# Feed-forward pairs of an encoder trunk: products joined in PSUM banks that ScalarE fills beforehand, in a new order

## The chip, the cores and the metric

One core of one Trainium2 chip runs the whole program. The metric is the device time of one execution in microseconds (us). The kernel before was run three times: 2769.55, 2768.38 and 2768.38 us, median 2768.38. The profile is one further execution, whose span from the first to the last instruction is 2767.2 us.

## The reference

Two sequences (512 and 256 tokens, 1024 wide) go through two layers with shared weights. Each layer is a feed-forward block, a token mixer and a second feed-forward block. There are thus four feed-forward blocks, and the change is in them alone.

```python
def swiglu_ffn(x, w1, w2):
    gate, up = jnp.split(x @ w1, 2, axis=-1)
    return (jax.nn.silu(gate) * up) @ w2

for li in range(DEPTH):
    x = x + 0.5 * swiglu_ffn(rmsnorm(x, norm_g[li, 0]), ffn_w1[li, 0], ffn_w2[li, 0])
    h = rmsnorm(x, norm_g[li, 1])
    ...
    x = x + mix
    x = x + 0.5 * swiglu_ffn(rmsnorm(x, norm_g[li, 2]), ffn_w1[li, 1], ffn_w2[li, 1])
```

Everything is in float32, `D_MODEL` is 1024 and `D_FF` is 2816, which is 22 columns of 128 hidden units.

## The kernel before, in words

**Tiling.** The 768 tokens of both sequences are handled together, in two halves of 384 (`H`). A float32 product is made of three matmuls: each operand is split into a rounded part and a remainder ("hi" and "lo"), and hi·hi, hi·lo and lo·hi are added up in PSUM. Splitting a weight takes a cast on ScalarE (L208), which gives hi, and a subtraction on VectorE (L209), which gives lo; for the product p5 of an up pair, GpSimd does the subtraction.

**Seven products instead of eight.** Most of the matmul work is done as a two-by-two block product by seven products p1 to p7 (Strassen's way, in Winograd's form). The first matrix is split by tokens and by the contracted dimension, the weights by gate/up and by the contracted dimension; the sums and differences of blocks that the seven products need are made beforehand. One column `j` of hidden units is one call of `up_pair`: seven products of 12 matmuls each (128x128 weights against 384 columns) into four PSUM banks a, b, c and d, and out come two tiles, silu(gate)·up of the two halves of the tokens. Columns 0 and 1 are done plainly (`up_plain`); the remaining 20 are pairs, so there are 80 pairs in the four blocks.

**Order in a block.** A block has five groups of four columns. After the columns of a group stands one `down_quad`: seven products with `w2`, each of 3 x 6 matmuls against 512 columns, 126 in all, whose results VectorE adds to the residual x (L599, by `add_x`). The down products run in the order `DOWN` = p1 p2 p5 p4 p7 p6 p3. p2, p4 and p3 run on in the banks of p1, p5 and p7, after VectorE has added what those banks held so far to x: p3 cannot begin in a bank of p7 before that addition. After the fifth group come the last two columns, as pairs, and their part of the down product (`add`).

**Weights.** `load_next` issues the loads on SP's queue into four raw buffers `wr` of 512 KB. For an up pair, raw buffer one holds blocks a11 and a12, buffer two holds a21 and a22. Three sums are made on the way: a DMA from GpSimd's queue adds a11 to a separately loaded block `s3` (for p7) and another adds a22 to a21 (`into`, L147); VectorE then makes a11 += a21 (the step "second" in the code) and a12 += a11 ("fourth"), both on L215. The table `UP` is the order in which an up pair's seven weights are staged; "second" and "fourth" are tied to a place in it by the dictionary `behind`. `ahead` stages as many weights as the eight buffers `w` hold: an up weight takes one of them, a down weight two, so a weight is staged up to eight products before it is used. It is called after each product, and behind a product's end its buffer comes free.

**Who sets the order.** The code emits operations in its own order; the framework then places them on each engine, where they run strictly in turn. `keep_in_program_order` holds "second" and "fourth" where the code has them. [...]

## Time and profile before

| what | value |
|---|---|
| median of three runs | 2768.38 us |
| span of the profiled execution | 2767.2 us |
| VectorE busy | 2206.5 us (80%), 3766 instructions |
| ScalarE busy | 1386.0 us (50%), 2589 instructions |
| GpSimd busy | 453.0 us (16%), 491 instructions |
| moved by DMA | 325.22 MB, 118 GB/s on average |
| mean granted TensorE clock | 0.999 |

How to read the rows: a group's row names the line of the code, the engine, the operation, what is written and read, and the count; then the busy time in us and the mean duration of one in ns; behind the second bar the time in which the engine was idle just before these instructions, and who ended the idle time. A row of waits names who waited for whom, with the total in us, the number of times and the longest. In the timeline a row gives the start in us, the duration in us, and in brackets the idle time before it.

### The profile page before, as it was taken

To read this page: it belongs to the slowest core of one execution; us is meant where nothing else is said; L and a number is where in the kernel's file an instruction comes from. 1 tells how busy PE (TensorE), PEld (TensorE's weight loads), DVE (VectorE), ACT (ScalarE), POOL (GpSimd) and SP (SyncE) were. 2 spreads that over 40 slices of the span, in tenths; PEclk is the share of its full clock that TensorE was granted. 3 is DMA by queue.
4 is the path that set the end of the run, shared out by engine and by line. 5 is a ranking of instruction groups with operands and counts; after the bars stand their busy time and mean duration, and the time that the engine had idled before them with its cause. 6 is when DMAs were issued, how large, how long until landed. Compare 5 with 4: busy or idle time off the path is not lost.

```text
span 2767.2 us, 40933 instructions
## 1 busy us (share of the span) xinstructions
PE 2745.0 (99%) x15117; PEld 2554.8 (92%) x15117; DVE 2206.5 (80%) x3766; ACT 1386.0 (50%) x2589; POOL 453.0 (16%) x491
## 2 busy tenths in 40 slices
PE   8999999999999999999999999999999999999998
PEld 8999999989999889999999999999888889999998
DVE  8788788767887888788878887887847868788877
ACT  7344444634455675444445543444458855444443
POOL 2111121200000101211111121111105611211111
PEclk9999999999999999999999999999999999999999
DMA  6554554851122743655444355544424422655443
GB/s 172 130 125 114 126 140 124 227 161 39 39 62 66 205 119 78 143 134 131 115 117 121 78 145 134 126 119 118 130 73 111 89 69 73 145 134 130 114 118 107
DMA packets 352040, 325.22 MB, mean 118 GB/s; under 512 B 14216, under 2 KB 271200, under 8 KB 351840
## 3 DMA queue, kind: packets, MB, share of 16 engines
q1 hardware_dynamic: 303040, 224.56, 27.7%
q0 software_dynamic: 44496, 84.56, 17.4%
q10 hardware_dynamic: 4304, 13.49, 1.3%
q8 instruction: 118, 1.93, 0.3%
q14 instruction: 82, 0.67, 0.1%
HBM read 225.82 MB, written 15.73 MB: 87 GB/s over the span
## 4 chain that ended last, share of the span: by engine, by line
PE 96%; DVE 2%; ACT 1%; DMA 1%; issue 0%; DVEq 0%; POOL 0%; SPq 0%; ACTq 0%; POOLq 0%
PE ps L513 42%; PE ps L577 21%; PE ps L315 6%; PE ps L316 6%; PE ps L314 6%; PE ps L760 5%; PE ps L823 3%; PE ps L928 1%; PE ps L1414 1%; PE ps L904 1%; PE ps L385 1%; PE ps L1426 0%; PE ps L1376 0%; PE ps L1427 0%; PE ps L1377 0%; PE ps L1181 0%
## 5 line engine op out<-in xcount | busy, mean ns | idle before, releaser
L513 PE MATMUL ps<-big,w 128*128 128x384 f32 x6720 | 1169.3, 334 | 0.0
L513 PEld LDWEIGHTS ps<-big,w 128*128 128x128 f32 x6720 | 1165.9, 188 | 1.7 <-ACT tA L530 0.2
L208 ACT CAST w<-wr 128x512 fp32r<-128x512 f32 x600 | 415.8, 707 | 689.2 <-PE ps L513 274.9
L577 PE MATMUL ps<-w,big 128*128 128x512 f32 x2520 | 575.7, 390 | 0.0
L577 PEld LDWEIGHTS ps<-w,big 128*128 128x128 f32 x2520 | 472.7, 188 | 98.0 <-ACT big L319 0.4
L209 DVE TENSOR_TENSOR w<-wr,w 128x512 fp32r<-128x512 f32 (+1 forms) x520 | 438.0, 846 | 145.9 <-ACT w L208 123.9
L147 POOL DMA_DIRECT2D s<-wr x126 | 109.8, 878 | 1250.3 <-DMA s<-in_ffn_w_dram 432.0
L599 DVE SCALAR_TENSOR_TENSOR x<-ps,x 128x512 f32<-128x512 f32 x468 | 302.4, 686 | 10.1 <-PE ps L316 10.0
L314 PE MATMUL ps<-big,w 128*128 128x384 f32 x640 | 219.6, 345 | 1.2 <-ACT w L175 0.9
L315 PE MATMUL ps<-big,w 128*128 128x384 f32 x640 | 215.7, 337 | 0.7 <-DVE big L320 0.7
L316 PE MATMUL ps<-big,w 128*128 128x384 f32 x640 | 214.6, 335 | 0.0
L319 ACT CAST big<-tA 128x384 fp32r<-128x384 f32 x296 | 148.0, 513 | 115.4 <-DVE tA L545 37.0
L147 POOL DMA_DIRECT2D wr<-wr x109 | 94.9, 871 | 518.3 <-DMA wr<-in_ffn_w_dram 165.9
L760 PE MATMUL ps<-w,big 128*128 128x512 f32 x756 | 177.1, 392 | 0.1
L320 DVE TENSOR_TENSOR big<-tA,big 128x384 fp32r<-128x384 f32 x296 | 168.0, 578 | 6.7 <-ACT big L319 4.7
L209 POOL TENSOR_TENSOR w<-wr,w 128x512 fp32r<-128x512 f32 x80 | 137.4, 1718 | 197.8 <-ACT w L208 195.8
L760 PEld LDWEIGHTS ps<-w,big 128*128 128x128 f32 x756 | 140.6, 188 | 29.1 <-DVE w L320 0.6
L215 DVE TENSOR_TENSOR wr<-wr,wr 128x512 f32<-128x512 f32 (+1 forms) x120 | 123.3, 1027 | 25.9 <-issue 23.6
L314 PE MATMUL ps<-w,big 128*128 128x512 f32 x336 | 134.6, 401 | 0.1
L316 PE MATMUL ps<-w,big 128*128 128x512 f32 x336 | 131.8, 392 | 0.5 <-DVE big L400 0.5
L315 PE MATMUL ps<-w,big 128*128 128x512 f32 x336 | 131.8, 392 | 0.0
L315 PEld LDWEIGHTS ps<-big,w 128*128 128x128 f32 x640 | 120.6, 188 | 2.0 <-DVE big L320 1.7
(214 smaller groups left out, 3504.0 us busy)
## 6 DMA issues: line engine op xcount, KB each, us to landing
wr<-in_ffn_w_dram SPq DMA_DIRECT2D x264, 512.0 KB, 4.0
s<-wr POOLq DMA_DIRECT2D x126, 256.0 KB, 4.8
s<-in_ffn_w_dram SPq DMA_DIRECT2D x120, 256.0 KB, 3.2
wr<-wr POOLq DMA_DIRECT2D x80, 256.0 KB, 3.8
wr<-in_hg_w_in_dram SPq DMA_DIRECT2D x32, 512.0 KB, 3.9
wr<-wr POOLq DMA_DIRECT2D x29, 512.0 KB, 4.6
spill<-x ACTq DMA_DIRECT2D x12, 512.0 KB, 4.0
kept<-big POOLq DMA_DIRECT2D x8, 768.0 KB, 9.7
```

Of the source, the lines that this page charges most:

```text
L147: self.nc.gpsimd.dma_start(out, src, accum_op=ALU.add)
L208: nc.scalar.copy(h, src)
L209: (eng or nc.vector).tensor_sub(l, src, h.bitcast(F32))
L314: nc.tensor.matmul(out, a[0], b[0], start=first, stop=False)
L315: nc.tensor.matmul(out, a[0], b[1], start=False, stop=False)
L316: nc.tensor.matmul(out, a[1], b[0], start=False, stop=last)
L319: self.nc.scalar.copy(hi, src)
L320: self.nc.vector.tensor_sub(lo, src, hi.bitcast(F32))
L513: self.nc.tensor.matmul(ps, a[x], b[y], start=first and k == 0 and i == 0, stop=k == 3 and i == 2, skip_group_check=True,)
L577: nc.tensor.matmul(ps, a[x], w[y], start=name == chain and kp == 0 and q == 0, stop=kp == 1 and q == 2, skip_group_check=True,)
L599: self.nc.vector.scalar_tensor_tensor(x, ps, c, x, ALU.mult, ALU.add)
L760: nc.tensor.matmul(ps, x[:, sl], y, start=fresh and k == 0 and q == 0, stop=k == 3 and q == 2, skip_group_check=True,)
```

## The change

The seven products of `up_pair` run in the order p1 p5 p6 p2 p7 p3 p4 instead of p1 p7 p2 p5 p4 p6 p3, and the results are joined differently. Before, every product or pair of products stood in a bank of its own, and VectorE joined them with five additions and subtractions, then two multiplications. Now ScalarE writes −p1 into bank b, and p6's matmuls add to it there; ScalarE copies that bank into bank c, and p7 and then p4 add to it there. VectorE is left with two subtractions and two multiplications per pair. ScalarE has six operations per pair instead of four. The first pair behind the plain columns takes the two banks in which the plain columns were made.

In staging, "second" moves from behind p5 to behind p1, and "fourth" from behind p4 to behind p2. The second half of the tokens now comes out of a pair first, and in the last columns the block (2, 0) is added ahead of (0, 1).

```diff
-UP = ("p1", "p7", "p2", "p5", "p4", "p6", "p3")
+UP = ("p1", "p5", "p6", "p2", "p7", "p3", "p4")
...
+    def seeded(self):
+        return self.wide.pop(0) if self.wide else self.ps(H)
...
-        behind = {"p5": "second", "p4": "fourth"} if up else {}
+        behind = {"p1": "second", "p2": "fourth"} if up else {}
...
+        if half and j == PLAIN - 1:
+            self.wide += pss
         return t
...
-        a, b, c, d = (self.ps(H) for _ in range(4))
-        v, w, t = (self.tmp(H) for _ in range(3))
+        a, d = (self.ps(H) for _ in range(2))
+        b, c = (self.seeded() for _ in range(2))
+        t, v, w = (self.tmp(H) for _ in range(3))
         p = lambda name, ps, first, last: self.product(key, name, FACTOR[name], ps, first, last)
         p("p1", a, True, False)
-        nc.scalar.copy(v, a)
+        nc.scalar.activation(b, a, AF.Copy, scale=-1.0)
         self.ahead()
-        p("p7", c, True, False)
-        nc.scalar.copy(w, c)
+        p("p5", d, True, False)
+        nc.scalar.copy(w, d)
+        self.ahead()
+        p("p6", b, False, True)
+        nc.scalar.copy(c, b)
+        nc.scalar.copy(v, b)
         self.ahead()
         p("p2", a, False, True)
-        nc.scalar.activation(a, a, AF.Silu)
+        nc.scalar.activation(t, a, AF.Silu)
         self.ahead()
-        p("p5", d, True, False)
-        nc.vector.tensor_sub(w, w, d)
+        p("p7", c, False, False)
+        nc.vector.tensor_sub(w, c, w)
+        self.ahead()
+        p("p3", d, False, True)
+        nc.vector.tensor_sub(v, d, v)
+        self.last_act = nc.scalar.activation(v, v, AF.Silu).ins
+        nc.vector.tensor_mul(w, v, w)
+        yield 1, w
         self.ahead()
         p("p4", c, False, True)
-        p("p6", b, True, True)
-        nc.vector.tensor_sub(v, v, b)
-        nc.vector.tensor_sub(t, c, v)
-        nc.vector.tensor_mul(t, t, a)
-        yield t
-        nc.vector.tensor_sub(w, w, v)
-        self.ahead()
-        p("p3", d, False, True)
-        nc.vector.tensor_add(v, v, d)
-        self.last_act = nc.scalar.activation(v, v, AF.Silu).ins
-        self.last_dve = nc.vector.tensor_mul(w, v, w).ins
-        yield w
+        self.last_dve = nc.vector.tensor_mul(t, c, t).ins
+        yield 0, t
         self.ahead()
...
-            for i, k in (((0, 0), (1, 0), (0, 1)), ((1, 1),))[b] if b < 2 else ((b, 0), (b, 1)):
+            for i, k in (((0, 0), (1, 0), (2, 0), (0, 1)), ((1, 1),), ((2, 1),))[b] if b < 3 else ((b, 0), (b, 1)):
```

Lines from L82 on stand lower in the code after the change, by 4 up to the pairs and by 7 from the down products on: L208, L209 and L215 become L212, L213 and L219, L319 and L320 become L323 and L324, L434 becomes L438, and L599 becomes L606.

Two places show what the change does to the queues. The first is VectorE in the second half of a down product, while the weights of the next group's first pair are staged; `wr_1411` and `wr_1412` are that pair's two raw buffers, `ps_1433` to `ps_1435` the three banks of the down product p7, `ps_1438` to `ps_1440` those of p6, and L215 on 128x512 with two buffers is "second". Before:

```order
L599 SCALAR_TENSOR_TENSOR x_1236_8687<-ps_1428_9980,x_1236_8687 128x512
L209 TENSOR_TENSOR w_1431_10014<-wr_1411_9853,w_1431_10014 128x512
L209 TENSOR_TENSOR w_1432_10017<-s3_1413_9857,w_1432_10017 128x512
L599 SCALAR_TENSOR_TENSOR x_1249_8769<-ps_1433_10020,x_1249_8769 128x512
L599 SCALAR_TENSOR_TENSOR x_1250_8771<-ps_1434_10028,x_1250_8771 128x512
L599 SCALAR_TENSOR_TENSOR x_1251_8773<-ps_1435_10036,x_1251_8773 128x512
L209 TENSOR_TENSOR w_1436_10044<-wr_1411_9853,w_1436_10044 128x512
L215 TENSOR_TENSOR wr_1411_9853<-wr_1411_9853,wr_1412_9855 128x512
L599 SCALAR_TENSOR_TENSOR x_1249_8769<-ps_1438_10051,x_1249_8769 128x512
```

The same place after the change, where the raw buffers are `wr_1514` and `wr_1515`, p7's banks `ps_1536` to `ps_1538`, and p6's first bank `ps_1541`:

```order
L606 SCALAR_TENSOR_TENSOR x_1234_8665<-ps_1531_10731,x_1234_8665 128x512
L213 TENSOR_TENSOR w_1534_10765<-wr_1514_10595,w_1534_10765 128x512
L606 SCALAR_TENSOR_TENSOR x_1247_8747<-ps_1536_10772,x_1247_8747 128x512
L219 TENSOR_TENSOR wr_1514_10595<-wr_1514_10595,wr_1515_10597 128x512
L606 SCALAR_TENSOR_TENSOR x_1248_8749<-ps_1537_10780,x_1248_8749 128x512
L606 SCALAR_TENSOR_TENSOR x_1249_8751<-ps_1538_10788,x_1249_8751 128x512
L213 TENSOR_TENSOR w_1539_10796<-wr_1514_10595,w_1539_10796 128x512
L213 TENSOR_TENSOR w_1540_10799<-wr_1514_10595,w_1540_10799 128x512
L606 SCALAR_TENSOR_TENSOR x_1247_8747<-ps_1541_10803,x_1247_8747 128x512
```

"Second" now stands ahead of the additions from the second and third bank of p7, where it stood behind all three. It stands so in all 20 down products.

The second place is ScalarE while the third pair of a group runs, when the sums of the two earlier pairs' hidden tiles (`mix`) are split too; `big` are split hidden tiles, `w` weights, `ps` banks. Before, from the copy of p1 on:

```order
L530 COPY tA_1490_10404<-ps_1486_10400 128x384
L208 CAST w_1493_10420<-s3_1464_10231 128x512
L319 CAST big_1480_10378<-tA_1471_10258 128x384
L533 COPY tA_1491_10405<-ps_1488_10402 128x384
L208 CAST w_1494_10436<-wr_1462_10227 128x512
L319 CAST big_1482_10386<-tA_1453_10122 128x384
L536 ACTIVATE ps_1486_10400<-ps_1486_10400 128x384
L208 CAST w_1495_10452<-wr_1463_10229 128x512
L319 CAST big_1483_10391<-tA_1472_10259 128x384
```

After, from the filling of bank b (L537) to that of bank c (L543):

```order
L537 ACTIVATE ps_1484_10375<-ps_1482_10373 128x384
L212 CAST w_1489_10393<-wr_1458_10201 128x512
L323 CAST big_1478_10359<-tA_1450_10098 128x384
L540 COPY tA_1488_10379<-ps_1483_10374 128x384
L212 CAST w_1490_10409<-wr_1457_10199 128x512
L323 CAST big_1479_10364<-tA_1466_10231 128x384
L323 CAST big_1480_10367<-tA_1468_10233 128x384
L323 CAST big_1481_10370<-tA_1448_10096 128x384
L543 COPY ps_1485_10376<-ps_1484_10375 128x384
```

L530 and L533 wrote temporaries in SBUF. L537 and L543 write the banks into which p6 and p7 add, and four casts of hidden tiles stand between them.

More of the change, by code (lines that the diff above doesn't have):

```diff
@@ L65, in __init__ @@
         self.uid = 0
+        self.wide = []
         self.deferred = []
@@ L610, in gather @@
             def gather(ts, kp):
-                self.mix(ts[0], ts[1], ts[2], ts[3], lambda name, src: put(name, src, kp))
+                self.mix(*(ts[i] for i in range(4)), lambda name, src: put(name, src, kp))
             if g == 0:
@@ L625, in ffn @@
                     continue
-                ts = []
+                ts = {}
                 for j in range(2):
-                    for half, t in enumerate(self.up_pair(tag, 4 * g + 2 * kp + j)):
-                        ts.append(t)
+                    for half, t in self.up_pair(tag, 4 * g + 2 * kp + j):
+                        ts[2 * j + half] = t
                         name = f"b{j}{half}"
@@ L637, in ffn @@
             hid = self.big([P, 2, T], F32R)
-            for half, t in enumerate(self.up_pair(tag, j)):
+            for half, t in self.up_pair(tag, j):
                 self.split(t, *(hid[:, i, half * H : (half + 1) * H] for i in range(2)))
```

## The prediction

> **What bounds the kernel now.** I read the page first, then who TensorE waits for, then TensorE in a stretch of two feed-forward blocks.
>
> ```profile
> span 2767.2 us, 40933 instructions
> PE 2745.0 (99%) x15117; PEld 2554.8 (92%) x15117; DVE 2206.5 (80%) x3766; ACT 1386.0 (50%) x2589; POOL 453.0 (16%) x491
> ```
>
> ```profile
> PE ps L116 <- DMA tB<-in_hg_g_norm_dram: 7.6, 1, 7.6
> PE ps L1376 <- ACT tA L1367: 1.3, 2, 1.1
> ...
> PE ps L1426 <- ACT tA L319: 0.2, 1, 0.2
> ```
>
> ```profile
> 1062.00:1987.00 925.00, 924.94 (x4936) 871.25 (x4935) 753.10 (x1204) 415.98 (x723) 147.37 (x146) 1.00 0.51 123
> L513 PE MATMUL ps<-big,w 128*128 128x384 f32 x6720 | 1169.3, 334 | 0.0
> ```
>
> TensorE is busy for all but 22.2 us of the span. It waits in twelve places, the longest for the first constants (7.6 us), then 1.3 us and less, and none of the twelve is a pair's matmul on L513. In the 925 us window of two feed-forward blocks TensorE is busy 924.94 us at a granted clock of 1.00. The 6720 matmuls of the pairs take 1169.3 us, 174 ns each, with no idle time before them. VectorE is busy 753.10 of the same 925 us, and nothing in the pairs waits for it for long. TensorE sets the time alone.
>
> **What the change removes.** The number of matmuls stays: seven products of 12, 80 times. Three VectorE operations per pair go and two ScalarE operations come.
>
> ```profile
> L543 DVE TENSOR_TENSOR tA<-tA,ps 128x384 f32<-128x384 f32 x80 | 44.1, 551 | 37.8 <-PE ps L513 37.6
> L539 DVE TENSOR_TENSOR tA<-tA,ps 128x384 f32<-128x384 f32 x80 | 44.1, 552 | 78.6 <-PE ps L513 78.6
> L533 ACT COPY tA<-ps 128x384 f32<-128x384 f32 x80 | 38.4, 480 | 83.2 <-PE ps L513 82.9
> L536 ACT ACTIVATE ps<-ps 128x384 f32<-128x384 f32 x80 | 38.0, 475 | 57.8 <-PE ps L513 57.8
> ACT tA L533 <- PE ps L513: 82.9, 76, 1.7
> ```
>
> VectorE loses 240 x 0.55 = 132 us, ScalarE gains 160 x 0.48 = 77 us. All of it lay beside matmuls: L539, L543 and L533 wait for TensorE (78.6, 37.8 and 83.2 us in all), not TensorE for them. So the saving is worth nothing on the path, and the extra 77 us on an engine that is 50% busy cost nothing in themselves. No copy from one bank to another stands in the trace; L536, which writes back to a bank, takes 475 ns, as long as L533 to SBUF, so I take 0.48 us.
>
> **What the change adds: three new waits.** TensorE now waits for two ScalarE operations in each pair, and VectorE's sum "second" moves ahead.
>
> *The filled banks.* p6 needs bank b, written after p1, and p5 (12 x 174 ns = 2.09 us) runs between. p7 needs bank c, written after p6, and p2 runs between. Each time ScalarE has 2.09 us for an operation of 0.48 us, so it may be late by 1.6 us. Of the 80 copies on L533, 76 found ScalarE already waiting for TensorE, so it follows a product at once nearly always. Cost nothing, where ScalarE is free. Where it isn't is the second rival below.
>
> *"Second" behind p1.* Here I look at the down products. The rows are from the timeline of one of the 20, which begins at 1265.60: VectorE's late part, three of its earlier rows, SP's issues of loads, the busy times in the first half (VectorE 14.30 of 14.30 us), then TensorE, GpSimd and ScalarE, and last a row of waits over the whole span.
>
> ```profile
> 1285.78 0.68 DVE L209 TENSOR_TENSOR w<-wr,w 128x512 fp32r<-128x512 f32 x1
> 1286.38 0.69 DVE L209 TENSOR_TENSOR w<-s,w 128x512 fp32r<-128x512 f32 x1
> 1286.98 1.88 DVE L599 SCALAR_TENSOR_TENSOR x<-ps,x 128x512 f32<-128x512 f32 x3
> 1288.77 0.69 DVE L209 TENSOR_TENSOR w<-wr,w 128x512 fp32r<-128x512 f32 x1
> 1291.83 0.69 DVE L215 TENSOR_TENSOR wr<-wr,wr 128x512 f32<-128x512 f32 x1 [2.37 <-issue]
> 1292.44 1.88 DVE L599 SCALAR_TENSOR_TENSOR x<-ps,x 128x512 f32<-128x512 f32 x3
> ```
>
> ```profile
> 1265.83 0.55 DVE L550 TENSOR_TENSOR tA<-tA,ps 128x384 f32<-128x384 f32 x1
> 1266.29 1.22 DVE L209 TENSOR_TENSOR w<-wr,w 128x1024 fp32r<-128x1024 f32 x1
> ...
> 1277.44 1.22 DVE L215 TENSOR_TENSOR wr<-wr,wr 128x1024 f32<-128x1024 f32 x1
> ```
>
> ```profile
> 1278.69 6.97 SPq L160 DMA_DIRECT2D wr<-in_ffn_w_dram  x3
> ```
>
> ```profile
> 1265.60:1279.90 14.30, 14.30 (x64) 11.82 (x64) 14.30 (x26) 5.66 (x10) 0.88 (x1) 1.00 0.26 74
> ```
>
> ```profile
> 1265.60 28.76 PE L577 MATMUL ps<-w,big 128*128 128x512 f32 x126
> 1294.20 2.09 PE L513 MATMUL ps<-big,w 128*128 128x384 f32 x11
> ```
>
> ```profile
> 1278.38 0.88 POOL L147 DMA_DIRECT2D s<-wr  x1 [20.59 <-DMA s<-in_ffn_w_dram]
> 1284.97 0.86 POOL L147 DMA_DIRECT2D wr<-wr  x1 [5.72 <-DMA wr<-in_ffn_w_dram]
> ```
>
> ```profile
> 1291.90 1.67 ACT L208 CAST w<-wr 128x512 fp32r<-128x512 f32 x3 [5.27 <-DMA wr<-wr]
> ```
>
> ```profile
> DVE wr L215 <- issue: 23.6, 13, 2.4
> ```
>
> The next pair's second raw buffer lands shortly before 1284.97, GpSimd then issues the DMA that adds a22 to a21, and this lands at about 1291.8, which releases ScalarE's cast of p5 (5.27 us idle) and VectorE's "second" (2.37 us idle). Before the change that wait hurt nobody, since the three additions from p7's banks were already done at 1286.98 to 1288.86. By the order after the change, "second" stands ahead of the additions from p7's second and third bank. TensorE needs these: p3 runs on in p7's banks. One matmul here takes (1294.20 − 1265.60) / 126 = 0.227 us, and p3's second bank begins after 114 of them, at 1265.60 + 25.88 = 1291.48.
>
> "Second" cannot start before its DMA lands. The chain to the landing begins at the down product's own "second", which ends at 1277.44 + 1.22 = 1278.66 and frees the raw buffer whose load is issued at 1278.69. VectorE is busy without a break up to there; after the change one operation on 384 columns fewer is queued ahead of it (L559 alone where L550 and L552 stood). The next operation starts 0.46 us behind one of these (1265.83, 1266.29), and a split will wait a little for its cast: I take 0.3 us earlier. With a wait of w us, "second" started at 1291.83 − 2.37 + w = 1289.46 + w in this group's clock, and now starts 0.3 us sooner; the next addition starts 0.61 us later (1292.44 − 1291.83) and takes 0.69. It ends at 1290.46 + w, and TensorE is held for 1290.46 + w − 1291.48 = w − 1.02 us. In this group, near the longest wait of 2.4, that is 1.35 us. The row of waits gives 13 such waits of 23.6 us together. If all were over 1.02 us, the sum is 23.6 − 13 x 1.02 = **10.3 us**. The third bank has 6 x 0.227 = 1.36 us more and its addition comes only 0.6 later, so it is not late again.
>
> Bounds: with no shift of the landing, the sum is 23.6 − 13 x 0.72 = 14.2 us. It falls if the landing comes still sooner, since the later s3 sums now stand behind GpSimd's p5 subtraction and take no share of the DMA while a21's sum is under way; if it came 1 us sooner in all, each wait would cost w − 1.72, at most 0.7 and with the mean w of 1.8 about 0.1 us, together some 2 us. I keep 2 and 14 as ends, and 10.3 as the value, since nothing moves the load itself.
>
> *Smaller moves.* The second pair of a group is the next to meet its sum of a21.
>
> ```profile
> 1293.86 0.86 POOL L147 DMA_DIRECT2D wr<-wr  x1
> 1297.83 1.29 DVE L209 TENSOR_TENSOR w<-wr,w 128x512 fp32r<-128x512 f32 x2
> ...
> wr<-wr POOLq DMA_DIRECT2D x80, 256.0 KB, 3.8
> ...
> L319 ACT CAST big<-tA 128x384 fp32r<-128x384 f32 x296 | 148.0, 513 | 115.4 <-DVE tA L545 37.0 <-DVE tA L552 36.2 <-DVE tA L423 16.4
> L320 DVE TENSOR_TENSOR big<-tA,big 128x384 fp32r<-128x384 f32 x296 | 168.0, 578 | 6.7 <-ACT big L319 4.7
> ```
>
> Issued at 1293.86 and 3.8 us under way, it lands at 1297.7, and p1 is split by 1299.1, so "second" finds it there or waits a little, and no addition of a down product stands behind it: nothing. "Fourth" waits for no DMA. The swapped halves at the end of a block need the last hidden tile after 18 matmuls, 18 x 0.227 = 4.1 us; its multiplication (as L539), cast and subtraction take 0.55 + 0.51 + 0.58 = 1.6 us: nothing.
>
> **Sum.** The profiled execution took 2767.2 us in its span, the median of the runs is 2768.38, 1.2 us around it. 2768.4 + 10.3 = 2778.7, forecast **2779 us**, 0.4% slower.
>
> **Rivals.**
>
> *The wait is absorbed.* If a21's sum lands a microsecond sooner, or VectorE's additions get ahead of it, the time stays at 2768 to 2773. For it: half of the down product has slack on VectorE, and 7 of the 20 sums already land early enough for no wait. Against it: the order of the instructions is fixed, and TensorE has no slack to take it from.
>
> *Bank c comes late as well.* In a group's third pair, four casts of hidden tiles stand ahead of L543 on ScalarE, and they wait for VectorE's chain L426, L427, L437, L438. I count from the pair's first matmul, with the durations above. Bank c may be filled from 6.3 us (p6's end) and must be by 4 x 2.09 = 8.36. The chain's last link ends at about 6.0, the casts behind it take three times 0.47 to about 7.5, and L543 ends at 8.0: 0.4 us to spare. But GpSimd's subtraction for p5 now falls beside this chain.
>
> ```profile
> 1157.19 2.57 DVE L215 TENSOR_TENSOR wr<-wr,wr 128x512 f32<-128x512 f32 x1
> 1157.58 1.62 POOL L209 TENSOR_TENSOR w<-wr,w 128x512 fp32r<-128x512 f32 x1
> ```
>
> Beside it, this operation of VectorE took 2.57 us instead of 0.69, 1.9 more. Of 1.9 us more in the chain, about 0.8 falls into time in which VectorE waits there for casts, and 0.4 is spare: L543 would be 0.7 us late, in 16 third pairs 11 us, and the time 2790. At the other end it costs nothing, and I take nothing, since most such operations are not stretched so far:
>
> ```profile
> L215 DVE TENSOR_TENSOR wr<-wr,wr 128x512 f32<-128x512 f32 (+1 forms) x120 | 123.3, 1027 | 25.9 <-issue 23.6 <-DVE w L209 2.4
> ```
>
> 40 of these at 1.22 us and 80 at 0.69 would take 104 us; 123.3 is 0.24 more for each of the 80.
>
> [...]
>
> *Faster.* VectorE, freed of 132 us, might bring forward what TensorE waits for between the blocks, where norms and transposes follow the last additions. TensorE's eleven waits behind the first constants, from 1.3 us down to 0.2 us in the rows above, come to 6.2 us together. If all of them went and no new wait came, the time would be 2762. It decides only if the new waits above are under 1 us in all. Against it: most of these waits lie in the mixers, which the change does not touch.
>
> **How the numbers follow.** A measurement of this kernel can tell about 0.2%, 5.5 us, from no change. "Second" holds p3 (2774 to 2783): 0.58. Both it and bank c late (over 2783): 0.10. Absorbed, or so little that it stays within 5.5 us: 0.27. Faster by more: 0.05. Slower is thus 0.68, no change 0.27, faster 0.05. For eight in ten I take 2767 to 2788: the low end leaves out the faster case, the high end the worst of both waits.
>
> **What would show it.** In the profile after, TensorE's waits must name L606 on VectorE, on the down products' matmuls, some 13 times at about 0.3 to 1.4 us, and VectorE's idle time before "second" must grow from 23.6 us, as it now sits there with nothing else to do in all 20 groups. VectorE should be busy about 2075 us and ScalarE about 1463. If TensorE waits on L519 for ScalarE, bank c or b is late. If TensorE's rows show no such waits and the time is unchanged, the landing came sooner, to be seen on ScalarE's wait for the DMA of the raw buffers. The forecast is wrong if TensorE's matmuls themselves change pace, since I took 174 ns for both.

## The result, and the profile after

| | before | after |
|---|---|---|
| median | 2768.49 us (2768.38 to 2769.55, 4 runs) | 2805.89 us (2802.28 to 2807.55, 4 runs) |
| ratio | | 1.0133, 95% interval 1.0119 to 1.0148 |
| profiled execution | 2767.2 us span | 2804.28 us, span 2802.2 us |

The changed kernel is 1.3% slower, 37 us. The forecast was 2779, and its range ended at 2788: the direction was right, and the size was not. From the page of the kernel after (the span, the engines, the matmuls of the pairs on L519 and of the down products on L584):

```profile
span 2802.2 us, 40756 instructions
...
PE 2759.8 (98%) x15117; PEld 2553.5 (91%) x15117; DVE 2134.8 (76%) x3526; ACT 1439.6 (51%) x2749; POOL 442.0 (16%) x491
...
L519 PE MATMUL ps<-big,w 128*128 128x384 f32 x6720 | 1175.3, 335 | 4.8 <-ACT ps L543 3.2
...
L584 PE MATMUL ps<-w,big 128*128 128x512 f32 x2520 | 581.3, 391 | 12.2 <-DVE x L606 12.1
```

And who TensorE waits for, the longest waits (us in total, times, longest):

```profile
PE ps L584 <- DVE x L606: 12.1, 16, 1.7
PE ps L120 <- DMA tB<-in_hg_g_norm_dram: 7.3, 1, 7.3
PE ps L519 <- ACT ps L543: 3.2, 3, 1.2
PE ps L519 <- DVE tA L550: 1.5, 2, 1.1
PE ps L1433 <- ACT tA L323: 1.5, 1, 1.5
```

VectorE has 240 operations fewer and ScalarE 160 more, as the change says. What is new is that TensorE waits: in the down products for VectorE's additions (L606), as the prediction named it, and in the pairs for bank c (L543). The rows of waits leave out short gaps. So I summed, over all matmuls, the time from one's start to the next one's start, by the line of the first: from the first matmul to the last it is 34.4 us more than before. Of this, 17.8 are in the down products and 10.8 in the pairs: 4.8 in the third pairs of 16 groups (0.3 each), 5.3 in the first pairs of the four blocks, 0.7 in one more. Another 5.4 are in the transposes on L389 (2.5), at and behind the ends of the feed-forward blocks, and in the products on L318 to L320 (2.9). Most of these 2.9 are one place in a mixer, where TensorE waits 1.49 us on L1433 instead of 0.20 (L1426 before) and then runs at half clock, a granted clock of 0.50, for 3.41 us (the clock is the third number from the end of a window's row):

```profile
2250.29:2253.70 3.41, 1.70 (x7) 0.85 (x5) 1.46 (x3) 2.08 (x4) 1.34 (x4) 1.00 0.22 20
2253.70:2257.11 3.41, 3.41 (x9) 2.64 (x9) 1.23 (x3) 0.12 (x1) 0.00 (x0) 0.50 0.00 0
```

**Where in a down product.** Not where I put it. One group of 20, VectorE's queue at the start of the down product, and TensorE's rows beside it:

```profile
1097.41 1.23 DVE L213 TENSOR_TENSOR w<-wr,w 128x1024 fp32r<-128x1024 f32 x1 [1.50 <-ACT w L212]
1098.55 0.55 DVE L553 TENSOR_TENSOR tA<-ps,tA 128x384 f32<-128x384 f32 x1
1099.69 0.56 DVE L555 TENSOR_TENSOR tA<-tA,tA 128x384 f32<-128x384 f32 x1 [0.59 <-ACT tA L554]
1100.17 0.55 DVE L559 TENSOR_TENSOR tA<-ps,tA 128x384 f32<-128x384 f32 x1
1100.83 0.56 DVE L324 TENSOR_TENSOR big<-tA,big 128x384 fp32r<-128x384 f32 x1
1101.31 1.22 DVE L213 TENSOR_TENSOR w<-wr,w 128x1024 fp32r<-128x1024 f32 x1
1102.44 0.55 DVE L324 TENSOR_TENSOR big<-tA,big 128x384 fp32r<-128x384 f32 x1
1102.91 0.55 DVE L426 TENSOR_TENSOR tA<-tA,tA 128x384 f32<-128x384 f32 x1
1103.38 0.68 DVE L606 SCALAR_TENSOR_TENSOR x<-ps,x 128x512 f32<-128x512 f32 x1
```

```profile
1099.31 4.28 PE L584 MATMUL ps<-w,big 128*128 128x512 f32 x18
1104.12 1.20 PE L584 MATMUL ps<-w,big 128*128 128x512 f32 x4 [0.53 <-DVE x L606]
```

TensorE stops after 18 matmuls: p1 is done in its three banks, and p2 runs on in the first of them, which VectorE must first add to x (1103.38, done at 1104.06). Over the 20 groups the step from the 18th to the 19th matmul takes 14.9 us more than its 0.23, the next one 2.1, and at p3's banks nothing. The addition is late because what stands ahead of it is: the subtraction at 1097.41 waited for ScalarE's cast, and that for a DMA.

The same start before the change, in the group that began its down product at 1091.87: four operations behind the pair's last matmul, then the addition, done 0.67 us ahead of the 19th matmul's turn:

```profile
1092.06 0.55 DVE L550 TENSOR_TENSOR tA<-tA,ps 128x384 f32<-128x384 f32 x1
1092.53 1.22 DVE L209 TENSOR_TENSOR w<-wr,w 128x1024 fp32r<-128x1024 f32 x1
1093.67 0.55 DVE L320 TENSOR_TENSOR big<-tA,big 128x384 fp32r<-128x384 f32 x1
1094.14 0.55 DVE L552 TENSOR_TENSOR tA<-tA,tA 128x384 f32<-128x384 f32 x1
1094.61 0.68 DVE L599 SCALAR_TENSOR_TENSOR x<-ps,x 128x512 f32<-128x512 f32 x1
```

The DMAs of the group after the change, with their issue times (a row `x2` is two issues, the second at its end): the load of the last `s3` block of the down product, the loads of its third and fourth raw buffer, GpSimd's two sums, and the cast that waits for the second sum:

```profile
1081.33 0.34 SPq L198 DMA_DIRECT2D s<-in_ffn_w_dram  x1
1082.39 2.32 SPq L164 DMA_DIRECT2D wr<-in_ffn_w_dram  x2
1084.52 0.87 POOL L151 DMA_DIRECT2D s<-wr  x1 [8.38 <-DVE w L213]
1091.74 0.85 POOL L151 DMA_DIRECT2D wr<-wr  x1 [6.34 <-DMA wr<-in_ffn_w_dram]
1096.32 2.20 ACT L212 CAST w<-wr 128x1024 fp32r<-128x1024 f32 x2 [2.50 <-DMA wr<-wr]
```

The same DMAs before the change, in that group (its down product begins 7.44 us earlier on the clock):

```profile
1067.00 0.34 SPq L194 DMA_DIRECT2D s<-in_ffn_w_dram  x1
1071.46 0.85 POOL L147 DMA_DIRECT2D s<-wr  x1 [3.68 <-PE ps L513]
...
1074.25 2.96 SPq L160 DMA_DIRECT2D wr<-in_ffn_w_dram  x2
1081.30 0.87 POOL L147 DMA_DIRECT2D wr<-wr  x1 [7.68 <-DVE w L209]
```

Before, the `s3` block was loaded 24.9 us ahead of the down product and its sum had landed when the fourth raw buffer was loaded. After, that block is loaded 18.0 us ahead, and its sum is issued at 1084.52, beside the fourth load, whose issue ends at 1084.71. The load now takes 6.7 us instead of 3.8, and the sum that needs it is issued 7.6 us ahead of the down product instead of 10.6. So the first reading was: there are two `s3` buffers, a buffer comes free when p7's weight is split, and the change moved p7 from second to fifth in the staging order. It moved a DMA, the DMA delayed another, and VectorE, whose order is fixed, carried the delay to p2.

### The profile page after: what moved, and what is told of

The parts are those of the page before. It is cut to its first block, busy times and chain, and to the rows that moved or that the text cites. A ratio compares the mean times of both kernels' runs of the same rounds, so it can differ in the third digit from the quotient of the medians.

```text
span 2802.2 us, 40756 instructions
## 1 busy us (share of the span) xinstructions
PE 2759.8 (98%) x15117; PEld 2553.5 (91%) x15117; DVE 2134.8 (76%) x3526; ACT 1439.6 (51%) x2749; POOL 442.0 (16%) x491
## 4 chain that ended last, share of the span: by engine, by line
PE 74%; DVE 10%; DMA 9%; ACT 4%; issue 2%; ACTq 0%; POOL 0%; DVEq 0%; POOLq 0%; SPq 0%
PE ps L519 30%; PE ps L584 17%; PE ps L319 5%; PE ps L320 5%; PE ps L318 5%; DMA wr<-in_ffn_w_dram 4%; PE ps L767 4%; DMA wr<-wr 3%; PE ps L830 3%; DVE w L213 3%; DVE big L324 2%; ACT w L212 1%; DVE x L606 1%; PE ps L1421 1%; ACT big L323 1%
## 5 line engine op out<-in xcount | busy, mean ns | idle before, releaser
L519 PE MATMUL ps<-big,w 128*128 128x384 f32 x6720 | 1175.3, 335 | 4.8 <-ACT ps L543 3.2
L519 PEld LDWEIGHTS ps<-big,w 128*128 128x128 f32 x6720 | 1165.4, 188 | 13.0 <-ACT ps L543 9.3
L212 ACT CAST w<-wr 128x512 fp32r<-128x512 f32 x600 | 416.1, 707 | 585.4 <-DVE wr L219 248.6
L584 PE MATMUL ps<-w,big 128*128 128x512 f32 x2520 | 581.3, 391 | 12.2 <-DVE x L606 12.1
L213 DVE TENSOR_TENSOR w<-wr,w 128x512 fp32r<-128x512 f32 (+1 forms) x520 | 441.1, 856 | 197.5 <-ACT w L212 130.5
L584 PEld LDWEIGHTS ps<-w,big 128*128 128x128 f32 x2520 | 470.6, 188 | 117.8 <-DVE x L606 20.4
L606 DVE SCALAR_TENSOR_TENSOR x<-ps,x 128x512 f32<-128x512 f32 x468 | 305.5, 681 | 13.7 <-PE ps L320 13.7
L318 PE MATMUL ps<-big,w 128*128 128x384 f32 x640 | 219.5, 345 | 1.7 <-ACT w L179 1.0
L319 PE MATMUL ps<-big,w 128*128 128x384 f32 x640 | 216.0, 337 | 1.0 <-DVE big L324 0.9
L320 PE MATMUL ps<-big,w 128*128 128x384 f32 x640 | 215.0, 336 | 0.0
L323 ACT CAST big<-tA 128x384 fp32r<-128x384 f32 x296 | 146.9, 512 | 126.6 <-DVE tA L426 44.4
L324 DVE TENSOR_TENSOR big<-tA,big 128x384 fp32r<-128x384 f32 x296 | 162.3, 560 | 25.1 <-ACT big L323 22.4
L767 PE MATMUL ps<-w,big 128*128 128x512 f32 x756 | 177.2, 393 | 0.1
L767 PEld LDWEIGHTS ps<-w,big 128*128 128x128 f32 x756 | 140.6, 188 | 29.1 <-DVE w L324 0.6
L213 POOL TENSOR_TENSOR w<-wr,w 128x512 fp32r<-128x512 f32 x80 | 121.8, 1523 | 280.0 <-ACT w L212 265.5
L151 POOL DMA_DIRECT2D wr<-wr x109 | 100.8, 925 | 387.0 <-DMA wr<-in_ffn_w_dram 153.2
L219 DVE TENSOR_TENSOR wr<-wr,wr 128x512 f32<-128x512 f32 (+1 forms) x120 | 117.3, 978 | 39.1 <-DMA wr<-wr 35.2
L318 PE MATMUL ps<-w,big 128*128 128x512 f32 x336 | 135.4, 403 | 1.3 <-ACT big L403 0.7
L319 PE MATMUL ps<-w,big 128*128 128x512 f32 x336 | 132.4, 394 | 0.0
L320 PE MATMUL ps<-w,big 128*128 128x512 f32 x336 | 132.4, 394 | 0.0
L319 PEld LDWEIGHTS ps<-big,w 128*128 128x128 f32 x640 | 120.6, 188 | 2.7 <-DVE big L324 2.6
```

The source lines that it names most:

```text
L151: self.nc.gpsimd.dma_start(out, src, accum_op=ALU.add)
L212: nc.scalar.copy(h, src)
L213: (eng or nc.vector).tensor_sub(l, src, h.bitcast(F32))
L318: nc.tensor.matmul(out, a[0], b[0], start=first, stop=False)
L319: nc.tensor.matmul(out, a[0], b[1], start=False, stop=False)
L320: nc.tensor.matmul(out, a[1], b[0], start=False, stop=last)
```

## The experiments

The theories: (1) the prediction's, that "second" in its new place holds the additions; (2) the late `s3` buffers; (3) GpSimd's subtraction for p5, which slows VectorE beside it; (4) for the 5.4 us, the order of the last additions. In the table, means over the 20 groups from each profile: from the issue to the landing of the fourth raw load, the landing of the sum on it ahead of the down product, the time lost over all groups at p2's first bank (18th matmul) and at p3's first bank (108th), and the time of all pairs' matmuls, start to start.

| kernel | 4th load | sum lands | lost at p2 | lost at p3 | pairs | median |
|---|---|---|---|---|---|---|
| before | 4.1 us | −5.1 us | 0.1 us | 0 us | 1165.5 us | 2768.5 us |
| after | 6.6 | −3.1 | 14.9 | 0 | 1176.3 | 2805.9 |
| e1 before, "second" behind p1 | 4.1 | −5.4 | 0 | 27.0 | 1165.4 | 2801.6 |
| e2 after, p7 staged second | 4.5 | −5.2 | 0 | 0.6 | 1166.6 | 2777.1 |
| e3 after, p5's subtraction on VectorE | 5.7 | −4.0 | 2.3 | 18.1 | 1165.5 | 2803.1 |
| e8 after, three `s3` buffers | 4.7 | −4.9 | 0.4 | 0 | 1180.3 | 2812.3 |
| e4 after, "second" behind p5 | 5.1 | −4.6 | 1.8 | 0 | 1172.2 | 2784.8 |
| e11 e4 and e3 together | 6.4 | −3.2 | 12.3 | 16.5 | 1169.3 | 2811.7 |
| e6 e2 and e4 together | 4.5 | −5.1 | 0.8 | 0 | 1165.3 | 2775.0 |
| e7 e6 with the old last additions | 4.6 | −5.0 | 1.0 | 0 | 1165.8 | 2774.4 |

**e1, "second" alone**, in the kernel before:

```diff
-        behind = {"p5": "second", "p4": "fourth"} if up else {}
+        behind = {"p1": "second", "p4": "fourth"} if up else {}
```

> The kernel before, with one part of the change alone: the sum "second" follows p1's split, as after the change, and "fourth", the order of the products, the seeds of the banks and everything else stay. First theory (the prediction's): "second" stands ahead of the additions from p7's second and third bank while the DMA that adds a22 to a21 still lands as late as before the change, so TensorE waits on VectorE's addition at p3's second bank (the matmul after 114 of a down product) in some 13 of 20 groups, 10 us together: 2778.7 us, 2770 to 2783 by the bounds of the prediction. Second theory (the buffers of the a11 sums): the 37 us of the change came from p7's later split, which frees the s3 buffers later and so moves DMAs; that part is not in this kernel, so no wait at p2's first bank (the matmul after 18) may appear here; for p3 this theory says the same as the first, since the landings are those of before. Rival: the additions get by, 2768 us.

Measured: 2801.62 us (2799.05 to 2808.03), ratio 1.0123 (1.0108 to 1.0138). VectorE and TensorE at the end of a down product, then the row of waits:

```profile
1122.84 0.69 DVE L215 TENSOR_TENSOR wr<-wr,wr 128x512 f32<-128x512 f32 x1 [2.78 <-issue]
1123.45 1.88 DVE L599 SCALAR_TENSOR_TENSOR x<-ps,x 128x512 f32<-128x512 f32 x3
```

```profile
1120.64 2.65 PE L577 MATMUL ps<-w,big 128*128 128x512 f32 x11
1124.28 4.36 PE L577 MATMUL ps<-w,big 128*128 128x512 f32 x18 [0.98 <-DVE x L599]
```

```profile
PE ps L577 <- DVE x L599: 23.1, 16, 2.5
```

The mechanism of the prediction is real, and dearer than it said. "Second" waits 2.8 us here (over all groups it starts 0.08 us behind the landing of the sum on a21), the additions from all three of p7's banks stand behind it (in the changed kernel only the last two do), and p3 is late in its first bank in every group. It costs 35.3 us in the down products: 27.0 at the 108th matmul and most of the rest in slow matmuls behind it (last section). The pairs are untouched.

**e2, p7 staged second**, the products still used in the new order:

```diff
-UP = ("p1", "p5", "p6", "p2", "p7", "p3", "p4")
+UP = ("p1", "p7", "p5", "p6", "p2", "p3", "p4")
```

> The changed kernel, with p7's split staged second instead of fifth (p1 p7 p5 p6 p2 p3 p4), the products in the order of the change. Second theory: the s3 buffers come free early again, s3's load and its sum with a11 lie ahead of the load of the down product's fourth raw buffer, which then takes some 3.8 us instead of 6.7; the sum on it lands 5 us before the down product instead of 3, VectorE's queue is on time, and the waits at p2's first bank (17.8 us in the down products) go: 2788 to 2791 us, if the next pair's sum doesn't become late in turn. If it does, "second" holds p3 as in the prediction, and the time is up to 10 us more, 2799. First theory ("second" alone costs): about 2806, no change, with the same waits. Third theory (GpSimd's subtraction of p5 beside VectorE's chain sets all): no change, 2806.

Measured: 2777.09 us (2776.94 to 2777.85), ratio 1.0031 (1.0019 to 1.0043). One tuple takes back 29 of the 37 us. From its page:

```profile
L519 PE MATMUL ps<-big,w 128*128 128x384 f32 x6720 | 1170.0, 334 | 0.4 <-DVE tA L550 0.4
...
L584 PE MATMUL ps<-w,big 128*128 128x512 f32 x2520 | 578.4, 391 | 0.4 <-ACT w L212 0.4
```

The `s3` load is back at 24.8 us ahead of the down product, the fourth load takes 4.5 us, and the waits at p2 are gone. The time is lower still than the 2788 to 2791 that theory 2 gave. The waits in the pairs went too, which I had not expected of it: theory 3 foretold no change, and theory 2 spoke of the down products alone.

**e8, three `s3` buffers**, the order untouched (seven `tA` temporaries instead of eight make the room):

```diff
-        tag, bufs, size = ("tA", 8, TA) if n > TB else ("tB", 2, TB)
+        tag, bufs, size = ("tA", 7, TA) if n > TB else ("tB", 2, TB)
...
-            t = self.wp.tile([P, 512], F32, tag="s3", name=self.name("s3"), bufs=2)
+            t = self.wp.tile([P, 512], F32, tag="s3", name=self.name("s3"), bufs=3)
```

> The changed kernel, with three s3 buffers instead of two, and seven of the tA temporaries instead of eight to make room; the order of everything is that of the change. Second theory: s3's second load for the down product no longer waits for the last pair's p7 split, its sum runs before the load of the fourth raw buffer, and the waits at p2's first bank go, 12 to 17 us: 2789 to 2794 us, or up to 10 us more if "second" then holds p3. First and third theory: 2806, the waits stay. If seven temporaries are too few, pairs would wait on a tA, which the profile would show as waits of ScalarE or VectorE for a buffer and on L519, and the time would be above 2806.

Measured: 2812.3 us (2810.12 to 2812.95), no gain in time, so the expected time was missed. The stage that it was made for did what theory 2 says:

```profile
L584 PE MATMUL ps<-w,big 128*128 128x512 f32 x2520 | 578.3, 390 | 0.1
```

The `s3` sum now comes 26.4 us ahead, the fourth load takes 4.7 us, and the down products take 15.1 us less than in the changed kernel. What ate it is elsewhere: 15.6 us more in the mixers (L767 waits for ScalarE in two places, 4.9 and 4.3 us, and runs slowly behind it), 4.0 in the pairs. This is the cleanest look at theory 2: in the feed-forward blocks no product has moved and VectorE's operations stand in the same order, and what differs is when an `s3` buffer is free.

**e3, p5's subtraction on VectorE**, and **e4, "second" behind p5**, each in the changed kernel, and **e11**, both:

```diff
-            split(name, own[name], nc.gpsimd if up and name == "p5" else None)
+            split(name, own[name], None)
```

```diff
-        behind = {"p1": "second", "p2": "fourth"} if up else {}
+        behind = {"p5": "second", "p2": "fourth"} if up else {}
```

> The changed kernel, with p5's subtraction on VectorE instead of GpSimd (80 operations of 0.69 us more on VectorE, none of 1.6 us on GpSimd). Third theory: VectorE's operations beside GpSimd's are no longer stretched, bank c is filled in time in the groups' third pairs, and their 16 waits of 0.4 us go, 6.3 us: 2799.5 us; if GpSimd's subtraction also delays the DMAs that GpSimd issues, more, down to 2790. Second theory: the waits at p2's first bank stay (their cause is the s3 buffers), 17.8 us within 3; the time 2798 to 2808. If bank c is late for ScalarE's own queue instead, 2806.

> The changed kernel, with "second" behind p5's split instead of p1's; all else as in the change, p7's split still fifth. First theory ("second" ahead of the additions costs in the changed kernel): its waits go and the time falls by some 10 us, to 2796 or less. Second theory (late s3 buffers, waits at p2's first bank): those waits stay at 15 us or so, since the down product's sum on its third raw buffer still lands about 3 us ahead of it; p3 was not waiting in the changed kernel, so nothing is gained there: 2801 to 2809. It may become slower if "second" behind p5 makes p6's split late for the pair.

> The changed kernel with "second" behind p5's split (2784.8 us) and p5's subtraction on VectorE instead of GpSimd; p7's split stays fifth. With "second" back the waits at p2's first bank are gone, and the pairs still take 6.7 us more than before the change, nearly all in the third pairs, at p7, which waits for bank c. Theory (GpSimd's subtraction stretches VectorE's chain of the hidden tiles, and so ScalarE's fill of bank c): these waits go, and the time is 2778 to 2779. Rival (ScalarE's own queue makes bank c late): they stay, 2785. If "second" comes ahead of one more addition of the down products by this, as with GpSimd's part alone, p3 waits and the time is above 2790.

Measured: e3 2803.13 us (2798.12 to 2804.2); e4 2784.83 (2783.67 to 2785.54), ratio 1.0058 (1.0044 to 1.0071); e11 2811.68 (2809.32 to 2813.62). First the pairs. The third pair of a group, in the changed kernel:

```profile
1161.27 1.28 POOL L213 TENSOR_TENSOR w<-wr,w 128x512 fp32r<-128x512 f32 x1 [0.79 <-ACT w L212]
1161.30 1.67 DVE L427 TENSOR_TENSOR tA<-tA,tA 128x384 f32<-128x384 f32 x1
```

And the same link of VectorE's chain over all groups, in the kernel before (L423), in the kernel after, in e4 (there it is the next link, L437) and in e11:

```profile
L423 DVE TENSOR_TENSOR tA<-tA,tA 128x384 f32<-128x384 f32 x40 | 22.2, 555 | 0.7
```

```profile
L427 DVE TENSOR_TENSOR tA<-tA,tA 128x384 f32<-128x384 f32 x40 | 40.9, 1022 | 0.7
```

```profile
L437 DVE TENSOR_TENSOR tA<-tA,tA 128x384 f32<-128x384 f32 x40 | 40.5, 1013 | 0.7
```

```profile
L427 DVE TENSOR_TENSOR tA<-tA,tA 128x384 f32<-128x384 f32 x40 | 22.1, 553 | 0.7
```

With GpSimd's subtraction beside it the operation takes 1.67 us instead of 0.55. ScalarE's casts wait for this chain, and bank c is filled behind them: 8.43 us into the pair, against 7.41 in e2 and e3. p7 was due at 8.32. It starts 0.05 us behind the filling, 0.16 late, and its next matmul is 0.11 later still: 0.3 us in each of 16 third pairs, 4.8 us (I had taken 0.4 and 6.3 in what e3 was to show). The first pair of a block is the third column of its group and meets the same chain: in three of the four, bank c is filled 9.4 to 9.6 us in, against 7.5 in e2 and e3, 4.0 us together. Without GpSimd's subtraction (e3, e11) these waits are gone. In e2, L427 takes 0.55 us too: p5 is staged one place later there and misses the chain. In e4 the third pairs are late at p4, by 0.2 us, and no longer at p7, other than e11's text has it. Theory 3 is right for the pairs, and wrong for the down products. (What e11 still loses in the pairs, 3.9 us, is in the last pair but one of each block.)

In the down products the three were surprises. VectorE's queue in e3, late in the down product that begins at 1098.25:

```profile
1121.94 0.69 DVE L213 TENSOR_TENSOR w<-wr,w 128x512 fp32r<-128x512 f32 x1 [3.32 <-ACT w L212]
1122.55 0.68 DVE L219 TENSOR_TENSOR wr<-wr,wr 128x512 f32<-128x512 f32 x1
1123.15 1.88 DVE L606 SCALAR_TENSOR_TENSOR x<-ps,x 128x512 f32<-128x512 f32 x3
```

e3 and e11 gained nothing in time, since p5's subtraction now stands in VectorE's queue, where it waits for its cast and so for the sum on a21. "Second" follows it, and all three additions of p7 stand behind both. p3 lost 18.1 and 16.5 us. In e2, too, "second" stands ahead of all three additions, but without that subtraction, and p3 lost 0.6. So e3's time lies in the range that theory 2 gave by luck: its waits at p2 were to stay and fell to 2.3 us. (The rows of waits name ScalarE's cast for p3 in e3. VectorE's addition ends 0.147 us ahead of p3 in e1, e3 and e11 alike.)

e4 was to stay above 2801 by theory 2 and to fall to 2796 by theory 1. It fell to 2784.8, and not by theory 1: p3 lost nothing to begin with, and in the down products "second" stands where it stood, ahead of the additions from p7's second and third bank, since p5's subtraction is not in VectorE's queue. What this version moves in VectorE's order lies nearly all in the third pairs. But the two DMAs now only half collide: the `s3` sum is issued 1.15 us behind the fourth load instead of 0.27, the load takes 5.1 us instead of 6.6, and a sum that lands 4.6 us ahead is just early enough. e3 and e11 are the test of this, as they move the same two DMAs again: with the `s3` sum 0.41 us ahead of the fourth load (e3) the load takes 5.7 us and p2 loses 2.3, with 0.17 us ahead (e11) 6.4 and 12.3. So theory 2 has to be mended. It isn't enough that the `s3` buffer is late, its sum has to fall onto the start of the fourth load. In every row of the table a load of 6.4 us and more goes with 12 to 15 us at p2, and one of 5.7 and less with at most 2.3. Why p7's split, and so the `s3` sum, comes at another moment in e3, e4 and e11 was not followed.

**e5, e6, e9, e7: what is left**, all with p7 staged second; e6 with "second" behind p5, e5 with the old order of the last additions, e9 as e5 with p5's subtraction on VectorE, e7 as e5 and e6:

```diff
-            for i, k in (((0, 0), (1, 0), (2, 0), (0, 1)), ((1, 1),), ((2, 1),))[b] if b < 3 else ((b, 0), (b, 1)):
+            for i, k in (((0, 0), (1, 0), (0, 1)), ((1, 1),))[b] if b < 2 else ((b, 0), (b, 1)):
```

> The changed kernel with p7's split staged second (2777.1 us), and the order of the last additions as before the change: (0,0) (1,0) (0,1) and (1,1), each block's later ones with its own turn. Theory: at the ends of the blocks the added step (2,0) stands ahead of (0,1) and of block 0's norm, so the transposes that follow start late; L389's matmuls took 2.5 us more than before and the first products behind them 0.7. Without it: 2774 to 2775 us. Rival: the swapped halves of the last pair set it, since (0,1) waits for the half that comes last, and the time stays at 2777.

> The changed kernel with p7's split staged second (2777.1 us), and "second" behind p5's split (third in that order) instead of p1's. Theory: with p7 staged second the additions from p7's banks end 23.7 to 24.6 us into the down product and p3 needs them at 24.5, so "second" has used up the room, and one group of 20 was late by 0.6 us; behind p5 that wait goes: 2776 to 2777. If "second" also delays the split of p5 or p1 in the pairs, more goes, down to 2774. Rival: nothing there, and p6's split becomes late in its turn: 2777 to 2785.

> The changed kernel with p7's split staged second, the order of the last additions as before, and p5's subtraction on VectorE instead of GpSimd, against the kernel with the first two alone. Theory: with GpSimd's subtraction gone nothing beside VectorE's chains is stretched, so the last 1.2 us of waits in the pairs go; in the down products "second" may come ahead of one more addition, as it did with p7 staged fifth (waits of 0.5 to 1.5 us at p3's first bank in all groups), which then costs up to 20 us. 2773 if it doesn't, 2785 to 2795 if it does.

> The changed kernel with p7's split staged second, "second" behind p5's split, and the order of the last additions as before: the three edits together. Theory: staging alone gave 2777.1, with "second" back 2775.0; the old order of the last additions took 1.9 us off L389's matmuls and 0.8 off the products behind them in its profile, though not off its median time, so between 2772 and 2775. What stays above the kernel before is the first addition of the down products, which stands 0.6 us later in VectorE's queue and leaves TensorE no room at p2's first bank (2.9 us in all). Rival: the order of the last additions is worth nothing, 2775.

Measured: e5 2777.14 us (2773.97 to 2778.4), e6 2775.04 (2774.15 to 2776.13), e9 2774.84 (2773.39 to 2776.29), e7 2774.41 (2772.68 to 2774.96), ratio 1.0020 (1.0011 to 1.0029). The old order of the last additions takes 1.9 us (e5) and 2.3 us (e7) off L389's transposes, so theory 4 holds there, but against e2 and e6 the medians move by no more than their spread (in e5's profile the pairs take 2.0 us more than in e2's). e9 is a miss of its dear end: with p7 staged second, p3 lost only 1.3 us. In e7 the down products still take 3.0 us more than before. No version of the change here beats the kernel before, and little was to be had: TensorE was busy 99% there.

**e10, the first pair's banks** from the pool instead of from the plain columns (`self.wide` stays empty). This changes what the first pair of a block computes; only its times are read.

> The changed kernel, with banks b and c of the first pair taken from the pool in turn like those of all other pairs, not from the plain columns. In the changed kernel TensorE waits 1.2 to 1.4 us in the first pair of each of the four blocks, 5.9 us together. Theory (the plain columns' banks are not the cause; GpSimd's subtraction and the late s3 sums are): the four waits stay, 2802 to 2809. Rival (they come from these banks, which the plain column's last multiplication reads): they go, 2800; or they were there to spare a wait, and the time is above 2809.

Measured: 2801.54 us (2798.87 to 2802.05). The four waits in the blocks' first pairs stay (1.0 to 1.3 us), and so do those at p2 (15.4 us): the plain banks are not their cause. Three of the four are the waits for bank c told above, and are gone in e2, e3 and e11. What the first block's wait hangs on, which comes at p4 and is gone in e3 and e11 too, wasn't followed.

## Why the prediction was wrong, point by point

**TensorE sets the time; VectorE's 132 us and ScalarE's 77 us are worth nothing.** Right. VectorE was freed of 240 operations and the time rose. The pairs' own rows changed by 131 and 77 us, as forecast. The page's busy times moved by less, to 2134.8 and 1439.6 instead of about 2075 and 1463, since rows that overlap are counted once there and L427 takes 19 us more. A copy from bank to bank takes 466 ns, against the 0.48 us that were taken.

**"Second" behind p1, 10.3 us, at p3.** The mechanism is right (e1), but in the changed kernel it costs nothing: p3 lost nothing. That the kernel is slower came out right by another wait, and so by luck. The sign that the prediction named came true all the same, 16 waits of the down products' matmuls for L606, longest 1.7 us, though they stand at p2. Only the place in the down product tells the two apart. In this kernel "second" starts 23.7 us into the down product on average, before the change 25.2, because the sum on a21 lands 1.5 us sooner. The prediction had that case in its bounds, "if it came 1 us sooner in all", and named its cause, the later `s3` sums. It followed them out of one place and not into the next.

**The step that failed** is the one that gave the down products a single term, 10.3 us at p3, "since nothing moves the load itself". The prediction checked the next pair's load and sum and left out the down product's own, and so had no term for p2. The change of `UP` moves p7's split by three places and, through the two `s3` buffers, a load by 7 us and its sum by as much, onto the fourth raw load. The sum behind that load lands 3.1 us ahead of the down product instead of 5.1, and p2 loses 14.9 us, 17.0 with the matmul behind it. This is most of the 17.8 us in the down products (e8 takes 15.1 of them back with the buffers alone).

**"One operation on 384 columns fewer is queued ahead."** This went the wrong way at the down product's start. By the rows above, five operations stand between the pair's last matmul and the first addition (L559, L324, L213, L324, L426) instead of four (L550, L209, L320, L552). L426 is the first link of the chain of the hidden tiles' sums. The first addition of p1 starts 3.35 us into the down product even where the DMA is early (e2, e4, e8), against 2.74 before, and p2 needs it done at 4.09; 0.67 us of room became 0.06. That alone costs little, about 3 us in e2, e6 and e7, but it left nothing against the late DMA.

**Filled banks b and c, 0; rival "bank c comes late as well", 11 us at a chance of 0.10.** The rival came true in its place and by its cause: 0.3 us per third pair instead of 0.7, 4.8 us, and 4.0 more in three blocks' first pairs, which it didn't count. Two of its terms were off. Its chain was stretched by 1.1 us, not 1.9, beside a subtraction of GpSimd of 1.28 us, not 1.62. And L543 had 0.9 us to spare, not 0.4: it ends 7.41 us into the pair in e2 and e3. In the rows above, GpSimd's row starts 0.03 us ahead of L427's and ends 1.25 us behind L427's start, and L427 took 1.67 us, 1.12 more than the 0.55 that it takes without GpSimd's subtraction (e3, e11). Taking nothing for it was the second mistake, since the prediction's own rows showed that such meetings happen, and staging p5 second put one into each group.

**Swapped halves and last additions, 0.** Wrong by a little: the transposes on L389 take 2.5 us more, of which the old order of the additions takes back 1.9 (e5) and 2.3 (e7). Of the 2.9 us on L318 to L320, 2.5 are the place in a mixer, the longer wait with the half clock behind it. TensorE waits there 1.85 us in e3 and 0.55 in e2, without a half clock in e2. Why ScalarE's split comes late there is open.

**The sum:** 17.8 (down products) + 10.8 (pairs) + 5.4 (transposes and L318 to L320) + 0.4 (all else) = 34.4 us from the first matmul to the last, of 35.0 in the spans.

## What to carry to other kernels

A table that sets the order in which weights are staged also sets when buffers come free, and so when DMAs start. Of a step that is moved, follow each buffer that it releases to the load that waits for it, and that load to whatever other DMA runs at its new time (here the load took 6.6 us instead of 4.1 beside a sum). Where the order on an engine is fixed, look for the consumers with the least room (0.67 us here) and ask what stands ahead of them: here the new order of the products took nearly all of it, which cost about 3 us alone (e2) and 18 together with a late DMA. And if a profile shows one operation stretched beside another engine's (here 1.67 us instead of 0.55), treat a move that puts the two side by side as a price to be paid, not as a rival of small chance.

## What the runs showed of the hardware that was not expected

**In e1 four waits of 2.00 to 2.55 us halved TensorE's clock and three of 2.07 to 2.32 did not: where they fell decided.** In e1 seven waits at p3 are of 2.0 us and more. Behind four of them (2.55, 2.00, 2.00, 2.46 us) the clock is halved, behind three (2.18, 2.07, 2.32) it isn't. TensorE's row behind one of the four:

```profile
2476.64 5.71 PE L577 MATMUL ps<-w,big 128*128 128x512 f32 x17 [2.00 <-DVE x L599]
```

The halved stretches begin at 196.53, 1623.30, 2476.63 and 2742.87 and last 3.41 us each, and the distances between them are whole multiples of 3.4133 us (418, 250 and 78). So I divide the span into stretches of 3.41 us from there. First the stretch that holds most of the wait of 2.18 us, which halved nothing, then the stretches ahead of, in and behind the halved one at 2476.63 (behind the length stands TensorE's busy time):

```profile
1473.12:1476.53 3.41, 1.78 (x8) 1.13 (x6) 0.89 (x2) 0.82 (x2) 0.19 (x2) 1.00 1.14 250
...
2473.22:2476.63 3.41, 1.42 (x7) 0.86 (x6) 1.43 (x3) 1.35 (x3) 0.72 (x2) 1.00 1.09 238
2476.63:2480.04 3.41, 3.40 (x8) 2.76 (x9) 3.41 (x7) 0.30 (x1) 1.46 (x2) 0.50 0.45 79
2480.04:2483.45 3.41, 3.41 (x17) 2.96 (x17) 3.41 (x7) 1.06 (x2) 0.00 (x0) 1.00 0.43 126
```

In e1 the clock is halved behind stretches in which TensorE was busy 0.95 to 1.47 us of 3.41, and stays at 1.00 behind those with 1.78 to 2.11. Of each of the four waits 1.9 us and more lies in one stretch; the other three straddle a border, and at most 1.6 us of each lies in one stretch. Around 1.7 us of busy time both occur: the clock fell behind 1.70 in the mixer of the changed kernel (first section), and not behind 1.66 in a stretch of e11. How this border depends on the matmuls wasn't looked into. The halved stretch adds about 1.6 us to such a wait: the 17 matmuls from 2476.64 on take 5.71 us, and behind the wait of 2.07 us, where the clock isn't halved, 18 take 4.36.

**In the changed kernel a late release cost 0.11 us more than the wait.** The matmul after the one that waited comes 0.11 us late as well, in the down products (2.1 us over the 20 groups) and at bank c alike, at a granted clock of 1.00. In e2, where p2 waits nowhere but VectorE's addition ends only 0.08 us ahead of it, that matmul still comes 0.08 us late (1.7 us over the groups). At bank c, with a wait of 0.16 us, this adds two thirds to the price.
